# Score products in two fp32r parts, and group pieces inside the value phase, in one layer of a hybrid attention and HGRN2 encoder

## The chip, the cores and the metric

One core of one Trainium2 chip runs the kernel. The metric is the time of one execution on the device in microseconds (us); lower is better. TensorE (PE) multiplies, VectorE (DVE), ScalarE (ACT) and GpSimd (POOL) work element by element, SyncE (SP) issues DMAs.

## The reference, cut to what matters

One layer over 1024 tokens of width 2048: normalise, project by a 2048 x 9216 matrix, run 16 attention heads and 8 HGRN2 heads side by side, gate, project back by `w_out`, add, and close with a gated embedding (`w_pg`, `w_pp`). The change touches the attention alone:

```python
q = rope_partial(heads(aq, ATT_HEADS), pos) * (ATT_HD ** -0.5)
k = rope_partial(heads(ak, ATT_HEADS), pos)
v = heads(av, ATT_HEADS)
res = [dilated_band_attention(q, k, v, w, d) for (w, d) in DILATION_CFG]
outs = jnp.stack([r[0] for r in res])
lses = jnp.stack([r[1] for r in res])
alpha = jax.nn.softmax(lses, axis=0)
o_att = jnp.einsum('gbsh,gbshe->bshe', alpha, outs).reshape(B, S, ATT_W)
y_att = o_att * jax.nn.silu(ag.astype(f32))
```

Each of the 16 heads (64 wide) is seen through three dilated windows, whose results are mixed by their softmax weights. The scores are wanted at float32 accuracy, so the kernel splits queries and keys into parts of lower precision and adds several products.

## The kernel before

The work runs in this order: the values of all heads (`v_group`, to about 360 us), the eight HGRN2 heads (to about 1290), the eight attention pairs of two heads (to about 2100), the output projection and the gated embedding.

A projection of 128 columns is a **group** (`group_parts`, L91 to L110): four weight pieces of 256 KB. Each piece is loaded by SP (L76), cast on ScalarE (`wh`, L83), its rest taken on GpSimd (`wl`, L84), and a bf16 copy made on VectorE (`wb`, L85); three buffers of each. It is written as a generator that yields twice a piece, so that a group can be spread over other work: the first part has 16 products of 512 columns of the high input half (L102, L103; fp32r) and 4 low ones (L107; bf16), the second part 4 low ones. Eight parts make a group, and a ninth call runs its sink, which reads the results out of two PSUM banks (four banks serve the groups, four the other work).

An attention **pair** has a query group, a key group and a gate group. The sinks of queries and keys (`rope_evac`) copy the bank to SBUF (`araw`, L521), turn it by four small DMAs (`apart`), a product on POOL (`apr`) and one on VectorE, and add (L558, L584). Then:

- `keys`, L555 to L574: the sum is split into three bf16 parts, one after the other: cast on ScalarE, subtract on VectorE, twice; the third cast is VectorE's. The two heads of the pair lie in the two halves of the partitions (`nat`), and each part is also copied into the other half by DMA (six copies of 64 KB a half of the tokens).
- `q_half(hf)`, L590 to L608: the queries of one half of the tokens are split likewise into `QT`, whose one buffer is free when the scores of the half before have been computed.
- `scores(hf)`, L626 to L683: eight units, four of stride 4 and wide reach and four local ones. A unit has three bf16 products for each head (L648), which contract both halves of the partitions, then the mask with a row minimum on VectorE (L657) and the exponential on ScalarE (L660). Local units first gather their queries (`aql`, L639), by turns on ScalarE and POOL. After every second unit the method takes one part of a group (`fill`). At its end come the factors of the softmax (L668 to L681).
- `values(hf)`, L685 to L728: eight turns; each scales the probabilities (L701, L703), transposes them on TensorE (L705) and copies them out of PSUM (L708); two turns later their V products run (L717, L720).

The loop at L817 to L836 sets the program order: scores of half 0 with gate parts between, four query parts of the next pair, `q_half(1)`, values of half 0, scores of half 1 with the other query parts, the keys of the next pair, its `q_half(0)`, values of half 1, the gate's other parts. The framework's scheduler takes this order as priority: an instruction whose operands and buffers it expects to be ready may be placed earlier on its engine. Within an engine the order is then fixed. Tiles of `h2` (five buffers of 128 x 512) hold the steps of queries and keys.

Of the kernel before, what the change touches and what calls it, by code (L numbers as in the profile page):

```python
# [13 lines left out]
F32R = mybir.dt.float32r  # L14
# [31 lines left out]
class Kern:  # L46
# [493 lines left out]
    class Pair:  # L540
# [7 lines left out]
        def keys(self):  # L548
            K, nat = self.K, self.nat
            nc = K.nc  # L550
            V = nc.vector
            self.KS = [K.big.tile([128, 2, S], BF16, name=f"ak{i}", tag=t, bufs=n)
                       for i, (t, n) in enumerate((("X", 2), ("X", 2), ("O", 1)))]

            def sink(hf, p):  # L555
                def fin(a, b):
                    kn = K.h2("akn")
                    V.tensor_tensor(kn.rearrange("p (r c) -> p c r", r=4), a.rearrange("p (c r) -> p c r", r=4),  # L558
                                    b.rearrange("p (c r) -> p c r", r=4), op=ALU.add)
                    a = kn  # L560
                    for s in range(3):
                        for h in range(2):
                            n, m = nat[h], nat[1 - h]
                            ks = self.KS[s][:, h].rearrange("p (r c) -> p r c", r=4)[:, :, 128 * hf:128 * hf + 128]
                            kd = ks[n]
                            an = a[n].rearrange("p (r c) -> p r c", r=4)
                            if s < 2:
                                nc.scalar.copy(kd, an)
                                V.tensor_tensor(an, an, kd, op=ALU.subtract)
                                nc.sync.dma_start(ks[m], kd)  # L570
                                if s == 0:
                                    nc.sync.dma_start(self.KS[2][m, h].rearrange("p (r c) -> p r c", r=4)[:, :, 128 * hf:128 * hf + 128], kd)
                            else:
                                V.tensor_copy(kd, an)  # L574
                K.rope_evac(False, hf, p, fin)
            return K.group_parts(self.w_in, 1024 + 128 * self.hp, sink)

# [12 lines left out]
        def q_half(self, hf):  # L590
            K, nat = self.K, self.nat
            nc = K.nc
            V = nc.vector
            q = self.qn[hf]
            QT = K.big.tile([128, 2, 2, 512], BF16, name="aqt", tag="hv", bufs=1)
            self.QT = QT
            for c in range(2):
                cs = slice(256 * c, 256 * c + 256)
                for h in range(2):
                    n = nat[h]  # L600
                    qd = QT[n, h, :, cs]
                    nc.scalar.copy(qd, q[n, None, cs].to_broadcast([64, 2, 256]))
                    V.tensor_tensor(q[n, cs], q[n, cs], QT[n, h, 0, cs], op=ALU.subtract)
                t = K.big.tile([128, 2, 256], BF16, name="aq23", tag="hacc", bufs=1)
                nc.scalar.copy(t[:, 0], q[:, cs])
                V.tensor_tensor(t[:, 1], q[:, cs], t[:, 0], op=ALU.subtract)
                for h in range(2):
                    nc.sync.dma_start(QT[nat[1 - h], h, :, cs], t[nat[h]])  # L608

        def loads(self):  # L610
            K, vsrc = self.K, self.vsrc
# [14 lines left out]
        def scores(self, hf, fill):  # L626
            K, KS, QT = self.K, self.KS, self.QT
            nc = K.nc
            V = nc.vector
            sm = [K.big.tile([128, 2, 4, 256], F32, name=f"asm{h}", tag=("F2", "Q2")[h], bufs=1) for h in range(2)]  # L630
            own = K.sp.tile([128, 2, 2, 2, 4], F32, name="aown", bufs=1)
            oth = K.sp.tile([128, 2, 2, 2, 4], F32, name="aoth", bufs=1)
            for u, (loc, i) in enumerate(((0, 0), (0, 1), (1, 0), (0, 2), (1, 1), (0, 3), (1, 2), (1, 3))):
                w0 = K.wstart(4 * hf + i)
                sc = K.wk("asc")
                if loc:
                    ql = K.big.tile([128, 4, 4, 32], BF16, name="aql", tag="aql", bufs=3)
                    src = QT.rearrange("p h s (r i b) -> p (h s) r i b", i=4, r=4)[:, :, :, i]
                    (nc.gpsimd.tensor_copy if i % 2 else nc.scalar.copy)(ql, src)  # L639
                for h in range(2):  # L640
                    for s, sq in ((0, 0), (1, 0), (2, 1)):
                        if loc:
                            st = ql[:, 2 * h + sq].rearrange("p r b -> p (r b)")
                            mv = KS[s][:, h].rearrange("p (r c) -> p r c", r=4)[:, :, w0 // 4:w0 // 4 + 64]
                        else:
                            st = QT[:, h, sq, 128 * i:128 * i + 128]
                            mv = KS[s][:, h, 256 * i:256 * i + 256]
                        nc.tensor.matmul(sc[:, 256 * h:256 * h + 256], st, mv, start=(h == 0 and s == 0),  # L648
                                         stop=(s == 2), skip_group_check=True)
                if loc:  # L650
                    ms = (w0 - 128 * (4 * hf + i)) // 4 + 32
                    mk = K.MK[:, 384:].rearrange("p (r c) -> p r c", r=4)[:, :, ms:ms + 64]
                else:
                    mk = K.MK[:, 128 - 128 * hf:384 - 128 * hf].rearrange("p (r c) -> p r c", r=4)
                for h in range(2):
                    d = sm[h][:, loc, i]
                    V.tensor_tensor_reduce(out=d.rearrange("p (r c) -> p r c", r=4),  # L657
                                           in0=sc[:, 256 * h:256 * h + 256].rearrange("p (r c) -> p r c", r=4), in1=mk, scale=1.0,
                                           scalar=3.0e38, op0=ALU.add, op1=ALU.min, accum_out=own[:, 0, loc, h, i:i + 1])
                    nc.scalar.activation(d, d, AF.Exp, scale=-1.0, bias=own[:, 0, loc, h, i:i + 1],  # L660
                                         accum_out=own[:, 1, loc, h, i:i + 1])
                if u % 2:
                    next(fill, None)
            for x in range(4):
                for y in range(4):
                    o = oth[32 * x:32 * x + 32].rearrange("p s l h i -> p (s l h) i")[:, :, y]
                    w = own[32 * y:32 * y + 32].rearrange("p s l h i -> p (s l h) i")[:, :, x]
                    V.tensor_copy(o, w)  # L668
            m = K.sp.tile([128, 2, 2, 4], F32, name="afm", bufs=1)
            e = K.sp.tile([128, 2, 2, 2, 4], F32, name="afe", bufs=1)  # L670
            for l in range(2):
                V.tensor_tensor(m[:, l], own[:, 0, l], oth[:, 0, 1 - l], op=ALU.min)
                V.tensor_tensor(e[:, 1, l], m[:, l], oth[:, 0, 1 - l], op=ALU.subtract)
            V.tensor_tensor(e[:, 0], m, own[:, 0], op=ALU.subtract)
            nc.scalar.activation(e, e, AF.Exp)
            V.tensor_tensor(own[:, 1], own[:, 1], e[:, 0], op=ALU.mult)
            for l in range(2):
                V.tensor_tensor(e[:, 1, l], e[:, 1, l], oth[:, 1, 1 - l], op=ALU.mult)
            V.tensor_tensor(m, own[:, 1], e[:, 1], op=ALU.add)
            V.reciprocal(m, m)  # L680
            V.tensor_tensor(m, m, e[:, 0], op=ALU.mult)  # L681
            self.sm[hf] = sm
            self.fac[hf] = m  # L683

        def values(self, hf):  # L685
            K, vn, vc, yt = self.K, self.vn, self.vc, self.yt
            nc = K.nc
            V = nc.vector
# [34 lines left out]
            for n in range(10):  # L723
                if n < 8:
                    turn(n)
                if n >= 2:
                    use(n - 2)
            nc.scalar.copy(yt[:, 512 * hf:512 * hf + 512].rearrange("p (i b r) -> p i r b", i=4, r=4), ov)  # L728
# [16 lines left out]
def tile_hybrid(ctx, tc, x, p, positions, w_in, w_out, g_pre, g_post, g_hg, lb_fwd, lb_bwd, w_pg, w_pp, g_ple, out):  # L745
# [54 lines left out]
    with tc.tile_pool(name="big", bufs=1) as big:  # L800
# [16 lines left out]
        for n, a in enumerate(heads):  # L817
            b = heads[n + 1] if n < 7 else None
            a.loads()
            g = a.gate()  # L820
            if n == 0:
                run(g, 4)
            a.scores(0, g)
            bq = b.queries() if b else iter(())
            run(bq, 4)
            if n == 7:
                run(g, 2)
            a.q_half(1)
            a.values(0)
            a.scores(1, bq if b else islice(g, 2))  # L830
            run(bq)
            if b:
                run(b.keys(), 9)
                b.q_half(0)
            a.values(1)
            run(g)  # L836
    fin = ctx.enter_context(tc.tile_pool(name="fin", bufs=1))
    Y = [fin.tile([128, 4, D], F32, name=f"Y{i}", tag=f"Y{i}") for i in range(2)]
# [256 lines left out]
```

## Time and profile before

| | |
|---|---|
| three runs, us | 2914.51, 2921.52, 2923.47 |
| median, us | 2921.52 |
| the profiled execution, us | 2914.93 |
| its span, first to last instruction, us | 2912.8 |
| mean granted TensorE clock | 0.987 |
| busy, PE / VectorE / ScalarE / GpSimd, us | 2745.8 / 1553.8 / 1019.0 / 1036.4 |

The span is what the trace covers; some 2 us lie around it. A page's L-number is the line of the kernel. A group of instructions is given as line, engine, operation, output<-inputs, shape and count, then busy time and the mean of one, then the idle time of the engine before it with what ended it. TensorE's weight loads are listed apart (PEld) and overlap the products.

### The profile page before, as it was taken

How to read it: one execution, taken by the hardware profiler on the slowest of the kernel's cores; microseconds unless marked ns; L12 is line 12 of the kernel's file. 1: busy time of each engine (PE TensorE's matmuls, PEld its weight loads, DVE VectorE, ACT ScalarE, POOL GpSimd, SP SyncE). 2: the span in 40 equal slices, each digit the busy share in tenths (PEclk: the TensorE clock that was granted, in tenths of full speed). 3: DMA queues.
4: the chain of work that ended last, by engine and by line, in shares of the span. 5: the costliest groups of instructions: out<-in, count | busy, mean ns of one | idle time of the engine just before them, and what ended most of it. 6: DMA issues, size and time to landing. Idle time of an engine off the chain costs nothing. (4 is left out here: it accounts for less than half of the span.)

```text
span 2912.8 us, 45468 instructions
## 1 busy us (share of the span) xinstructions
PE 2745.8 (94%) x17117; PEld 1898.4 (65%) x17360; DVE 1553.8 (53%) x3265; ACT 1019.0 (35%) x2094; POOL 1036.4 (36%) x801
## 2 busy tenths in 40 slices
PE   6999999999999999999899999999899999999997
PEld 4666666676677676676666666666666566566664
DVE  8601116856346346355756566666645635555555
ACT  5311112222122112125556555555633233333323
POOL 3422223313313313322222222233244554666555
PEclk9999999999999999999999999999999999999998
DMA  6412221211111111121222231232344543443453
GB/s 225 122 55 80 76 87 38 66 52 39 57 52 45 51 52 44 53 69 51 77 63 62 71 82 51 66 86 73 98 135 131 161 146 95 127 121 111 145 155 106
DMA packets 279899, 253.08 MB, mean 87 GB/s; under 512 B 46848, under 2 KB 203520, under 8 KB 278528
## 3 DMA queue, kind: packets, MB, share of 16 engines
q1 hardware_dynamic: 270512, 241.24, 28.7%
q10 hardware_dynamic: 9168, 8.93, 0.9%
q8 instruction: 136, 2.23, 0.3%
q14 instruction: 83, 0.68, 0.1%
HBM read 208.16 MB, written 29.36 MB: 82 GB/s over the span
## 5 line engine op out<-in xcount | busy, mean ns | idle before, releaser
L84 POOL TENSOR_TENSOR wl<-raw,wh 128x512 fp32r<-128x512 f32 x568 | 763.6, 1348 | 1580.4 <-ACT wh L83 1528.4
L85 DVE CAST wb<-raw 128x512 bf16<-128x512 f32 x584 | 427.0, 734 | 757.8 <-PE gb L107 252.8
L83 ACT CAST wh<-raw 128x512 fp32r<-128x512 f32 x584 | 358.1, 617 | 1199.1 <-PE gb L102 391.5
L102 PE MATMUL gb<-uh,wh 128*128 128x512 f32 x1792 | 746.0, 416 | 10.3 <-ACT araw L521 6.7
L103 PE MATMUL gb<-uh,wl 128*128 128x512 f32 x1792 | 710.2, 396 | 0.0
L107 PE MATMUL gb<-ul,wb 128*128 128x512 bf16 x1643 | 407.9, 380 | 8.9 <-issue 1.4
L102 PEld LDWEIGHTS gb<-uh,wh 128*128 128x128 f32 x1792 | 338.5, 189 | 99.2 <-ACT araw L521 9.6
L103 PEld LDWEIGHTS gb<-uh,wl 128*128 128x128 f32 x1792 | 338.7, 189 | 69.6
L107 PEld LDWEIGHTS <-wb 128*128 128x128 bf16 x1792 | 157.3, 98 | 207.0 <-issue 57.7
L877 PE MATMUL gb<-wh,yh 128*128 128x512 f32 x512 | 231.1, 452 | 5.7 <-DVE sg L738 4.3
L877 PE MATMUL gb<-wh,th 128*128 128x512 f32 x480 | 214.5, 447 | 0.0
L878 PE MATMUL gb<-wl,yh 128*128 128x512 f32 x512 | 203.4, 398 | 6.3 <-POOL wl L84 6.3
L878 PE MATMUL gb<-wl,th 128*128 128x512 f32 x480 | 189.2, 394 | 6.3 <-POOL wl L84 6.3
L660 ACT ACTIVATE asm<-asm,aown 128x256 f32<-128x256 f32 x256 | 126.9, 498 | 36.7 <-DVE aown L657 36.0
L881 PE MATMUL gb<-wb,yl 128*128 128x512 bf16 x481 | 135.6, 386 | 1.4
L881 PE MATMUL gb<-wb,tl 128*128 128x512 bf16 x452 | 125.3, 382 | 1.0
L877 PEld LDWEIGHTS gb<-wh,yh 128*128 128x128 f32 x512 | 97.8, 191 | 36.6 <-DVE sg L738 5.2
L776 PE MATMUL gb<-wh,uh 128*128 128x512 f32 x256 | 116.6, 462 | 1.4 <-ACT wh L83 1.3
L878 PEld LDWEIGHTS gb<-wl,yh 128*128 128x128 f32 x512 | 97.5, 190 | 27.7 <-POOL wl L84 8.8
L777 PE MATMUL gb<-wl,uh 128*128 128x512 f32 x256 | 102.4, 407 | 9.3 <-POOL wl L84 8.1
L877 PEld LDWEIGHTS gb<-wh,th 128*128 128x128 f32 x480 | 90.8, 189 | 27.2 <-ACT sg L981 2.0
L878 PEld LDWEIGHTS gb<-wl,th 128*128 128x128 f32 x480 | 90.4, 188 | 26.3 <-POOL wl L84 8.9
(287 smaller groups left out, 3798.8 us busy)
## 6 DMA issues: line engine op xcount, KB each, us to landing
raw<-in_w_in_dram SPq DMA_DIRECT2D x320, 256.0 KB
raw<-in_w_out_dram SPq DMA_DIRECT2D x128, 256.0 KB
raw<-in_w_pg_dram SPq DMA_DIRECT2D x128, 256.0 KB
xt<-in_x_dram SPq DMA_DIRECT2D x8, 1024.0 KB
vD<-vo SPq DMA_DIRECT2D x32, 256.0 KB
raw<-yD SPq DMA_DIRECT2D x32, 256.0 KB
xr<-in_x_dram SPq DMA_DIRECT2D x32, 256.0 KB
avn<-vD SPq DMA_DIRECT2D x32, 192.0 KB
```

Source lines behind the costliest of these rows:

```text
L83: nc.scalar.copy(wh, raw)
L84: (sub or nc.gpsimd).tensor_tensor(wl, raw, f32(wh), op=ALU.subtract)
L85: nc.vector.tensor_copy(wb, raw)
L102: nc.tensor.matmul(pb[hf], wh[:, k], self.uh[hf][:, kt], start=(kt == 0), stop=False)
L103: nc.tensor.matmul(pb[hf], wl[:, k], self.uh[hf][:, kt], start=False, stop=False)
L107: mm = nc.tensor.matmul(pb[hf], wb[:, k], self.ul[hf][:, kt], start=False, stop=(kt == KT - 1))
L660: nc.scalar.activation(d, d, AF.Exp, scale=-1.0, bias=own[:, 0, loc, h, i:i + 1], accum_out=own[:, 1, loc, h, i:i + 1])
L776: nc.tensor.matmul(pb[t], hi, wh, start=(k == 0), stop=False)
L777: nc.tensor.matmul(pb[t], hi, wl, start=False, stop=False)
L877: nc.tensor.matmul(pb[t], a, pc[0], start=first, stop=False)
L878: nc.tensor.matmul(pb[t], a, pc[1], start=False, stop=False)
L881: nc.tensor.matmul(pb[t], lo[:, k, 128 * t:128 * t + 128], pc[2], start=False, stop=last)
```

## The change

Queries and keys are split into two fp32r parts (a rounded one and the rest) in place of three bf16 ones. For each head, one key tile holds the high part in one half of the partitions and the low part in the other, and two query tiles hold the high part, and the low part, in both halves; so two products of 128 contracted rows give all four partial products. All rows of these tiles are written by DMA from the split tiles. The local query copies become two for a unit, one on ScalarE and one on POOL. `values` takes a generator and calls it after turns 1 and 5; the loop hands it query or gate parts, and two gate parts move ahead of the next pair's keys.

```diff
--- before.py
+++ after.py
@@ -549,29 +549,21 @@
             K, nat = self.K, self.nat
             nc = K.nc
             V = nc.vector
-            self.KS = [K.big.tile([128, 2, S], BF16, name=f"ak{i}", tag=t, bufs=n)
-                       for i, (t, n) in enumerate((("X", 2), ("X", 2), ("O", 1)))]
+            self.KS = [K.big.tile([128, S], F32R, name=f"ak{h}", tag="X", bufs=2) for h in range(2)]
 
             def sink(hf, p):
                 def fin(a, b):
                     kn = K.h2("akn")
                     V.tensor_tensor(kn.rearrange("p (r c) -> p c r", r=4), a.rearrange("p (c r) -> p c r", r=4),
                                     b.rearrange("p (c r) -> p c r", r=4), op=ALU.add)
-                    a = kn
-                    for s in range(3):
-                        for h in range(2):
-                            n, m = nat[h], nat[1 - h]
-                            ks = self.KS[s][:, h].rearrange("p (r c) -> p r c", r=4)[:, :, 128 * hf:128 * hf + 128]
-                            kd = ks[n]
-                            an = a[n].rearrange("p (r c) -> p r c", r=4)
-                            if s < 2:
-                                nc.scalar.copy(kd, an)
-                                V.tensor_tensor(an, an, kd, op=ALU.subtract)
-                                nc.sync.dma_start(ks[m], kd)
-                                if s == 0:
-                                    nc.sync.dma_start(self.KS[2][m, h].rearrange("p (r c) -> p r c", r=4)[:, :, 128 * hf:128 * hf + 128], kd)
-                            else:
-                                V.tensor_copy(kd, an)
+                    kh = K.h2("akh")
+                    nc.scalar.copy(kh.bitcast(F32R), kn)
+                    V.tensor_tensor(kn.bitcast(F32R), kn, kh, op=ALU.subtract)
+                    for h in range(2):
+                        n, m = nat[h], nat[1 - h]
+                        dst = f32(self.KS[h]).rearrange("p (r c) -> p r c", r=4)[:, :, 128 * hf:128 * hf + 128]
+                        nc.sync.dma_start(dst[n], kh[n].rearrange("p (r c) -> p r c", r=4))
+                        nc.sync.dma_start(dst[m], kn[n].rearrange("p (r c) -> p r c", r=4))
                 K.rope_evac(False, hf, p, fin)
             return K.group_parts(self.w_in, 1024 + 128 * self.hp, sink)
 
@@ -591,21 +583,15 @@
             K, nat = self.K, self.nat
             nc = K.nc
             V = nc.vector
-            q = self.qn[hf]
-            QT = K.big.tile([128, 2, 2, 512], BF16, name="aqt", tag="hv", bufs=1)
-            self.QT = QT
-            for c in range(2):
-                cs = slice(256 * c, 256 * c + 256)
+            q = self.qn.pop(hf)
+            self.QT = [K.big.tile([128, 2, 512], F32R, name=f"aqt{i}", tag=t, bufs=1) for i, t in enumerate(("hv", "O"))]
+            qh = K.h2("aqh")
+            nc.scalar.copy(qh.bitcast(F32R), q)
+            V.tensor_tensor(q.bitcast(F32R), q, qh, op=ALU.subtract)
+            for sq, src in ((0, qh), (1, q)):
                 for h in range(2):
-                    n = nat[h]
-                    qd = QT[n, h, :, cs]
-                    nc.scalar.copy(qd, q[n, None, cs].to_broadcast([64, 2, 256]))
-                    V.tensor_tensor(q[n, cs], q[n, cs], QT[n, h, 0, cs], op=ALU.subtract)
-                t = K.big.tile([128, 2, 256], BF16, name="aq23", tag="hacc", bufs=1)
-                nc.scalar.copy(t[:, 0], q[:, cs])
-                V.tensor_tensor(t[:, 1], q[:, cs], t[:, 0], op=ALU.subtract)
-                for h in range(2):
-                    nc.sync.dma_start(QT[nat[1 - h], h, :, cs], t[nat[h]])
+                    for o in range(2):
+                        nc.sync.dma_start(f32(self.QT[sq])[nat[o], h], src[nat[h]])
 
         def loads(self):
             K, vsrc = self.K, self.vsrc
@@ -634,19 +620,22 @@
                 w0 = K.wstart(4 * hf + i)
                 sc = K.wk("asc")
                 if loc:
-                    ql = K.big.tile([128, 4, 4, 32], BF16, name="aql", tag="aql", bufs=3)
-                    src = QT.rearrange("p h s (r i b) -> p (h s) r i b", i=4, r=4)[:, :, :, i]
-                    (nc.gpsimd.tensor_copy if i % 2 else nc.scalar.copy)(ql, src)
+                    ql = []
+                    for sq in range(2):
+                        tag, n = ("hacc", 1) if i % 2 and sq else ("aql", 3)
+                        ql.append(K.big.tile([128, 2, 4, 32], F32R, name="aql", tag=tag, bufs=n))
+                        src = f32(QT[sq]).rearrange("p h (r i b) -> p h r i b", i=4, r=4)[:, :, :, i]
+                        (nc.gpsimd.tensor_copy if sq else nc.scalar.copy)(ql[sq], src)
                 for h in range(2):
-                    for s, sq in ((0, 0), (1, 0), (2, 1)):
+                    for sq in range(2):
                         if loc:
-                            st = ql[:, 2 * h + sq].rearrange("p r b -> p (r b)")
-                            mv = KS[s][:, h].rearrange("p (r c) -> p r c", r=4)[:, :, w0 // 4:w0 // 4 + 64]
+                            st = ql[sq][:, h].rearrange("p r b -> p (r b)")
+                            mv = KS[h].rearrange("p (r c) -> p r c", r=4)[:, :, w0 // 4:w0 // 4 + 64]
                         else:
-                            st = QT[:, h, sq, 128 * i:128 * i + 128]
-                            mv = KS[s][:, h, 256 * i:256 * i + 256]
-                        nc.tensor.matmul(sc[:, 256 * h:256 * h + 256], st, mv, start=(h == 0 and s == 0),
-                                         stop=(s == 2), skip_group_check=True)
+                            st = QT[sq][:, h, 128 * i:128 * i + 128]
+                            mv = KS[h][:, 256 * i:256 * i + 256]
+                        nc.tensor.matmul(sc[:, 256 * h:256 * h + 256], st, mv, start=(h == 0 and sq == 0),
+                                         stop=(sq == 1), skip_group_check=True)
                 if loc:
                     ms = (w0 - 128 * (4 * hf + i)) // 4 + 32
                     mk = K.MK[:, 384:].rearrange("p (r c) -> p r c", r=4)[:, :, ms:ms + 64]
@@ -682,7 +671,7 @@
             self.sm[hf] = sm
             self.fac[hf] = m
 
-        def values(self, hf):
+        def values(self, hf, fill):
             K, vn, vc, yt = self.K, self.vn, self.vc, self.yt
             nc = K.nc
             V = nc.vector
@@ -723,6 +712,8 @@
             for n in range(10):
                 if n < 8:
                     turn(n)
+                if n in (1, 5):
+                    next(fill, None)
                 if n >= 2:
                     use(n - 2)
             nc.scalar.copy(yt[:, 512 * hf:512 * hf + 512].rearrange("p (i b r) -> p i r b", i=4, r=4), ov)
@@ -823,16 +814,16 @@
             a.scores(0, g)
             bq = b.queries() if b else iter(())
             run(bq, 4)
-            if n == 7:
-                run(g, 2)
             a.q_half(1)
-            a.values(0)
-            a.scores(1, bq if b else islice(g, 2))
+            a.values(0, bq if b else g)
+            a.scores(1, bq if b else islice(g, 1))
             run(bq)
             if b:
+                if n:
+                    run(g, 2)
                 run(b.keys(), 9)
                 b.q_half(0)
-            a.values(1)
+            a.values(1, islice(g, 1 if n == 7 else 2) if n else iter(()))
             run(g)
     fin = ctx.enter_context(tc.tile_pool(name="fin", bufs=1))
     Y = [fin.tile([128, 4, D], F32, name=f"Y{i}", tag=f"Y{i}") for i in range(2)]
```

## The prediction

> **What bounds the kernel now.** I read the page's busy times first, then the attention stage alone, since every edit lies in it: one row of the table of stretches, then the groups of TensorE instructions inside it.
>
> ```profile
> PE 2745.8 (94%) x17117; PEld 1898.4 (65%) x17360; DVE 1553.8 (53%) x3265; ACT 1019.0 (35%) x2094; POOL 1036.4 (36%) x801
> ...
> 1338.59:2034.34 695.75, 649.73 (x3910) 462.87 (x3964) 445.35 (x1315) 393.04 (x951) 179.85 (x151) 0.98 0.25 67
> ...
> L102 PE MATMUL gb<-uh,wh 128*128 128x512 f32 x649 | 273.1, 421 | 10.3 <-ACT araw L521 6.7 <-DVE sg L738 3.5
> L103 PE MATMUL gb<-uh,wl 128*128 128x512 f32 x650 | 259.2, 399 | 0.0
> ...
> L648 PE MATMUL asc<-ak,aql 128*128 128x256 bf16 x336 | 46.3, 284 | 5.1 <-DVE aown L657 5.1
> L648 PE MATMUL asc<-ak,aqt 128*128 128x256 bf16 x336 | 45.5, 276 | 12.2 <-DMA ak<-ak 12.2
> ```
>
> TensorE is busy 94% of the whole, and the stretch from the first score product of pair 0 to that of pair 7 (seven pairs, 695.75 us) shows the same: 649.73 us of TensorE against 445 of VectorE and 393 of ScalarE. But busy time counts each product's modelled end, so I price TensorE by the distance between starts, from the order of time (columns: start, duration of the merged run, instruction, count).
>
> ```profile
> 1402.86 0.39 PE L103 MATMUL gb<-uh,wl 128*128 128x512 f32 x1
> ...
> 1405.60 0.39 PE L103 MATMUL gb<-uh,wl 128*128 128x512 f32 x1
> ...
> 1400.89 1.90 PE L107 MATMUL gb<-ul,wb 128*128 128x512 bf16 x8
> ...
> 1563.78 1.48 PE L648 MATMUL asc<-ak,aqt 128*128 128x256 bf16 x12
> ...
> 1412.75 0.66 PE L705 MATMUL apt<-ident,asm 128*128 128x128 f32 x4
> 1413.34 0.66 PE L717 MATMUL ao<-aPT,avn 128*64 128x128 f32 x8
> ...
> 504.50 0.30 PEld L386 LDWEIGHTS pout<-hvt,ATT 128*128 128x128 f32 x2
> 504.72 0.30 PEld L388 LDWEIGHTS pout<-hst,Q 128*128 128x128 f32 x2
> ```
>
> Twelve steps of high products (fp32r, 512 columns) take 2.74 us: 0.228 each. Eight bf16 products of 512 columns take 1.90 less one duration of 0.38, over seven steps: 0.217. Twelve bf16 score products (256 columns) take 1.48 less one of 0.27, over eleven: 0.110. Four transposes, and the eight instructions of one turn's V products, take 0.59 each. For the seven pairs that is 1299 x 0.228 = 296, half as many low products at 0.217 = 141, 672 x 0.110 = 74, and 112 turns x (0.59 + 0.59) = 132: 643 us of the 696. So this stage is TensorE's own work plus some 53 us in which it is held up or slowed. Who holds it up:
>
> ```profile
> PE asc L648 <- DMA ak<-ak: 14.0, 8, 3.2
> PE apt L705 <- DVE asm L703: 8.7, 4, 2.7
> PE ao L717 <- ACT aPT L708: 8.6, 5, 2.0
> PE gb L102 <- ACT araw L521: 6.7, 7, 1.0
> PE asc L648 <- DVE aown L657: 5.8, 5, 1.8
> PE gb L877 <- DVE sg L738: 4.3, 2, 2.4
> PE gb L102 <- DVE sg L738: 3.5, 1, 3.5
> PE ao L720 <- DVE aPT L708: 2.9, 7, 0.8
> ```
>
> That is the list of waits of TensorE from 1290 to 2090 us (total, times, longest). The first score product of a pair waits for key copies (14.0), V products wait for the transposes' copies out of PSUM (8.6 + 2.9), the first key matmul waits until the query bank is emptied (6.7). The rest of the 53 is the clock, 0.98 over the stretch (14 us), and small steps.
>
> **1. Score products.** Per unit, six bf16 products go and four fp32r products of the same 256 columns come; 128 units in all (two halves x eight units x eight pairs). Now 6 x 0.110 = 0.66 us. No row shows an fp32r product of 256 columns. Lower end: half of the 512-column step, 0.114. The pout rows support it: two loads of 128x128 four-byte weights in 0.22 us, so such a load can follow another in 0.11. Upper end: the load's own duration, 189 ns in the load rows of L102 (98 for bf16), if nothing hides it. I take the bf16 step plus what 512-column fp32r costs over bf16: 0.110 + 0.011 = 0.121, since the load of 189 ns is evidently hidden there to within 11 ns. 4 x 0.121 = 0.48; 0.18 x 128 = **23 us less**. Ends: 0.114 gives 26 less; 0.189 gives 0.76, 13 us more. It falls on the path, because the stage is TensorE's.
>
> The load row weighs against this change, and so does a rule. The Trainium skill, "TensorE: Matmul & The Clock Gate", section "Weight-path perf modes — Fast Weight Load (FWL) and DoubleRow", says the quick weight load is for types other than FP32. The two load durations, 98 and 189 ns, agree. By the rule taken strictly, with 256 columns too few to hide such a load, the term would be the upper end, 13 us more.
>
> **2. Pieces between transposes and V products.** `values` gets two parts of a group: after turn 1 a large one (16 high, 4 low products: 4.5 us), after turn 5 a small one (0.9). The first V products then come 4.5 us after their transposes, where the longest wait was 2.0. I take the 8.6 and most of the 2.9 as gone: **11 us less**. The 8.7 us of transposes waiting for the factors lie ahead of the part, so I leave them. Next late is nothing in `values`: its turns run at 0.59 + 0.59 already.
>
> **3. Queries end earlier.** With two parts in `values(0)`, the queries' last parts and their copy out of PSUM fall inside `scores(1)`, and for pairs 1 to 6 two gate parts (5.4 us) stand before the keys. The wait for `araw` goes at six of seven places: **6 us less**. If the cover went, it would be back at 1 us each.
>
> **4. Key and query preparation.** The rows of groups (count, busy, mean ns, idle before):
>
> ```profile
> L568 ACT CAST ak<-akn 64x512 bf16<-64x512 f32 x64 | 39.5, 617 | 42.1 <-DVE akn L558 31.0 <-DVE akn L569 10.1
> L569 DVE TENSOR_TENSOR akn<-akn,ak 64x512 f32<-64x512 f32 x64 | 58.8, 918 | 15.9 <-ACT ak L568 14.6
> L574 DVE CAST ak<-akn 64x512 bf16<-64x512 f32 x32 | 23.3, 727 | 1.0
> L605 ACT CAST aq<-aq 128x256 bf16<-128x256 f32 x32 | 12.8, 401 | 35.7 <-DMA aqt<-aq 34.1 <-DVE aq L603 1.6
> L639 ACT COPY aql<-aqt 128x512 bf16<-128x512 bf16 x32 | 18.2, 616 | 34.5 <-DMA aqt<-aq 34.5
> ...
> L83 ACT CAST wh<-raw 128x512 fp32r<-128x512 f32 x584 | 358.1, 617 | 1199.1 <-PE gb L102 391.5
> L84 DVE TENSOR_TENSOR wl<-raw,wh 128x512 fp32r<-128x512 f32 x16 | 14.2, 890 | 3.0 <-ACT wh L83 3.0
> ```
>
> A half of keys costs VectorE 4 x 0.92 + 2 x 0.73 = 5.1 us now and one 0.89 after; ScalarE 4 x 0.62 and then one. Queries shrink alike, and ScalarE no longer stands 34 us behind the single buffer of L605. None of it is TensorE's, so off the path it is worth nothing by itself. What it shortens is this chain (pair 2's):
>
> ```profile
> 1601.71 1.24 PE L107 MATMUL gb<-ul,wb 128*128 128x512 bf16 x5
> ...
> 1602.26 0.59 ACT L521 ACTIVATE araw<-gb 128x512 f32<-128x512 f32 x1
> ...
> 1611.14 0.61 ACT L521 ACTIVATE araw<-gb 128x512 f32<-128x512 f32 x1
> ...
> 1616.74 0.70 SPq L525 DMA_DIRECT2D apart<-araw  x1
> ...
> 1625.16 1.08 DVE L558 TENSOR_TENSOR akn<-araw,apr 128x512 f32<-128x512 f32 x1
> ...
> 1632.17 0.44 PE L648 MATMUL asc<-ak,aqt 128*128 128x256 bf16 x2 [2.37 <-DMA ak<-ak]
> ```
>
> From the last key product (1602.8) to the first score, 29.4 us pass: the second half's `araw` is copied at 1611, its rotation is queued on SP behind six key copies, and the split follows from 1626. Afterwards the split is one cast and one subtraction (1.5 us, not two such steps in each of six pieces) and four copies for six; I count the chain 2 to 8 us shorter. But every key row now comes by DMA, 128 KB a copy (64 before), and the cover shrinks: two gate parts that stood behind `values(1)` now stand before the keys, 5.4 us at each of six transitions. The net I take at 1 us lost each: **6 us more**; ends, 14 less (the whole wait goes) and 32 more (6 x 5.4).
>
> SP issues four more copies a pair (24 for 20) at 0.6 to 0.7 us: covered by `values(0)` and the query parts at `q_half(1)`, by the 21 us of key matmuls at `q_half(0)`. Raw weight loads stand behind them on SP; a q_half of eight issues is 5 us, and three raw buffers hold 16 us of matmuls, so nothing. The second-half local query tiles must wait for earlier products, on POOL as now:
>
> ```profile
> POOL aql L639 <- PE asc L648: 28.8, 9, 8.2
> ```
>
> That wait reaches no TensorE row today. Copies double in number and halve in elements (0.40 us by L605); behind a POOL copy stands the subtraction of a weight piece, hidden by the same buffers: nothing. In pair 7 the gate's last small part moves into `values(1)`, and the output stage, which waits for its banks (4.3), may start 3 us earlier or later: nothing.
>
> **Sum.** -23 - 11 - 6 + 6 = **-34 us**. The profiled execution took 2914.93 us (span 2912.8 and 2 around it), the fastest end of the runs; their median, 2921.52, is 6.6 higher. The forecast for the median is 2921.5 - 34 = **2887 us**, its own range 2870 to 2905.
>
> **Rivals.** A: the loads bound the products (0.189): 13 more instead of 23 less, 2923 us, no change. For it, the load rows; against it, the 11 ns of step 1 and the pout rows. This is the Trainium skill's rule on quick loads at work.
>
> B, slower: **the keys come late**. Place: the first score product of pairs 2 to 7. Price: 5.4 us of lost cover at six transitions, 32, and the clock. A wait of 3.5 us after 1428 was followed by this (last columns: granted clock, DMA share, GB/s):
>
> ```profile
> 1430.00:1435.00 5.00, 3.26 (x7) 2.17 (x7) 4.77 (x7) 3.09 (x6) 1.27 (x1) 0.60 0.78 186
> 1435.00:1440.00 5.00, 4.13 (x16) 2.72 (x16) 3.89 (x9) 2.35 (x5) 2.39 (x2) 0.50 0.69 186
> ```
>
> 2.0 + 2.5 = 4.5 us of clock lost, 27 at six places. Then -23 - 11 - 6 + 32 + 27 = +19: 2940 us. It decides once the chain does not shorten while the cover does; the larger copies at a DMA share already 0.7 to 0.8 speak for it, against it that the program's order pulls later gate pieces before the scores (3.4 pieces lie between in pair 2, where two were written). The Trainium skill, same page, Part 1, has the clock halve after an idle window of about 3.4 us; the trace agrees with its 0.50.
>
> C: only the products pay, and moved pieces leave as much wait elsewhere: 2898 us. D: the relief of VectorE and ScalarE removes the waits for factors and keys and half the clock's 14 as well: -34 - 6 - 14 - 7 = -61, 2860 us. E: fp32r gains nothing from 256 columns, 0.228 a product, 32 us more for 23 less: 2942 us; the change then does not do what it says.
>
> **Chances.** Forecast 0.48, A 0.10, B 0.13, C 0.15, D 0.10, E 0.04. Faster by over 0.3% (9 us, about what a measurement of this kernel can tell from no change): forecast, C and D with a little lost at the edge, 0.72; within, A and edges, 0.11; slower, B and E, 0.17. The range 2862 to 2930 leaves out B, E and part of D: near 0.2.
>
> **What would show it.** Step 1: L648's successors 512 in number, about 0.12 us apart; at 0.19 it is A. Step 2: the waits of L717 and L720 gone. Step 3: no wait for `araw` at L102. Step 4: the wait of the first score below 3 us a pair; over 5 us with a clock near 0.5 behind it is B. The forecast is wrong if the order of instructions on TensorE changes so that pieces run out before scores.

## The result, and the profile after

| | before | after |
|---|---|---|
| median of six runs each, taken together, us | 2917.47 | 2904.23 |
| lowest to highest, us | 2914.51 to 2923.47 | 2899.36 to 2906.73 |
| profiled execution, us (its span) | 2914.93 (2912.8) | 2900.24 (2898.5) |
| mean granted TensorE clock | 0.987 | 0.984 |

The ratio is 0.9948, with a 95% interval of 0.9934 to 0.9963: the change makes the kernel faster by 13 us, about 0.5%. The forecast was 34 us faster (2887 us); the time lies inside the range, and the gain is well under half of the forecast one. Each ratio below is to the kernel before as timed beside that run, with medians from 2911.24 to 2915.96 us.

Of the changed kernel's page, the busy times (engine, us, share, instructions); its table of stretches for the attention stage, from the first score product to the last V product, which is the same stretch as the row of before below it (start and end, length, busy PE, PEld, DVE, ACT, POOL, clock, DMA share, GB/s):

```profile
PE 2726.5 (94%) x16853; PEld 1893.5 (65%) x17104; DVE 1449.1 (50%) x3105; ACT 951.3 (33%) x1998; POOL 1047.7 (36%) x833
```

```profile
1341.96:2097.70 755.74, 694.30 (x4069) 500.22 (x4136) 399.45 (x1340) 384.80 (x994) 207.59 (x198) 0.97 0.34 90
```

```profile
1338.59:2098.20 759.61, 704.67 (x4298) 501.75 (x4356) 491.80 (x1482) 441.25 (x1070) 192.55 (x162) 0.98 0.26 69
```

VectorE lost 92 us of work in the stage and ScalarE 56, yet the stage is only 4 us shorter. (Some more of the output projection now falls inside it, so what follows the stage is shorter by about 14.) The list of TensorE's waits from 1290 to 2090 us (engine, tile, line, what it waited for: total, times, longest) answers to the one shown of before:

```profile
PE gb L102 <- DMA aqt<-aqh: 19.7, 4, 5.6
PE apt L694 <- DVE asm L692: 16.3, 10, 2.2
PE asc L637 <- DMA aqt<-aqh: 9.5, 1, 9.5
PE gb L102 <- DVE sg L729: 4.4, 1, 4.4
PE asc L637 <- DMA aqt<-aq: 3.4, 2, 3.1
```

The waits of V products (8.6 and 2.9) and the wait for `araw` (6.7) are gone, as forecast. The wait for key copies (14.0), which was forecast to grow a little, is off the list too, but the query copies are issued behind the key copies and may hide it. In their place stand waits put down to the copies of the *query* tiles: 19.7 + 9.5 + 3.4 = 32.6 us at seven places, where before had none. The transposes' wait for the softmax factors nearly doubled, from 8.7 to 16.3.

The transition that ends with the first score at 1630 shows one of the new waits. (It is that of pair 3, counted from 0, and the same one as the prediction's chain to 1632, which is there called pair 2's; the lines are of the same place.) Of all engines' instructions in order of time, those that matter (start, duration of the merged run, instruction, count, idle time before it and what ended it):

```profile
1588.56 2.18 DVE L576 TENSOR_TENSOR aq<-araw,apr 128x512 f32<-128x512 f32 x1 [2.40 <-POOL apr L528]
...
1621.70 0.62 ACT L560 CAST akh<-akn 128x512 fp32r<-128x512 f32 x1 [3.68 <-DMA avn<-vD]
1622.23 0.62 ACT L589 CAST aqh<-aq 128x512 fp32r<-128x512 f32 x1
...
1622.83 1.90 PE L107 MATMUL gb<-ul,wb 128*128 128x512 bf16 x8
...
1626.94 1.28 ACT L728 ACT_TABLE_LOAD   x1 [3.52 <-DMA ak<-akh]
...
1628.36 2.54 SPq L594 DMA_DIRECT2D aqt<-aq  x4
...
1629.62 0.50 PE L102 MATMUL gb<-uh,wh 128*128 128x512 f32 x1 [4.88 <-DMA aqt<-aqh]
1630.20 0.77 PE L637 MATMUL asc<-ak,aqt 128*128 128x256 f32 x2
```

The later of the two query sums was ready at 1590.7 (1588.56 + 2.18), but the cast that begins the query split (L589) ran only at 1622.2, right behind the cast of the second key half, with no wait of ScalarE between the two. The same holds at all seven transitions. Its eight copies were issued until 1630.9. TensorE had run out of gate parts by then and stood still for 4.9 us. The clock followed:

```profile
1625.00:1630.00 5.00, 0.38 (x1) 0.19 (x1) 1.33 (x3) 2.37 (x3) 0.30 (x1) 1.00 0.84 223
1630.00:1635.00 5.00, 4.92 (x20) 4.18 (x20) 1.06 (x2) 1.23 (x3) 2.96 (x4) 0.66 0.77 239
```

The label "DMA aqt<-aqh" at L102 needs care. L102 there is the first product of the next gate group. It reads no query tile; it needs the bank that the old gate's sink empties, and that sink's sigmoid (L728) stood 3.5 us until a key copy out of `akh` had landed: it writes an `h2` tile too. So two things are late at one place: the gate's sink, and the first score, whose query copies were still being issued then. Both write `h2` tiles; whether that is what holds them, the experiments have to show.

### The profile page after: what moved, and what is told of

It reads as the page before. It is cut to its first block, busy times and chain, and to the rows that moved or that the text cites. A ratio compares the mean times of both kernels' runs of the same rounds, so it can differ in the third digit from the quotient of the medians.

```text
span 2898.5 us, 45014 instructions
## 1 busy us (share of the span) xinstructions
PE 2726.5 (94%) x16853; PEld 1893.5 (65%) x17104; DVE 1449.1 (50%) x3105; ACT 951.3 (33%) x1998; POOL 1047.7 (36%) x833
## 5 line engine op out<-in xcount | busy, mean ns | idle before, releaser
L85 DVE CAST wb<-raw 128x512 bf16<-128x512 f32 x584 | 406.6, 699 | 817.2 <-PE gb L107 311.8
L102 PE MATMUL gb<-uh,wh 128*128 128x512 f32 x1792 | 743.2, 415 | 24.3 <-DMA aqt<-aqh 19.7
L102 PEld LDWEIGHTS gb<-uh,wh 128*128 128x128 f32 x1792 | 339.9, 190 | 110.0 <-DVE sg L729 27.0
```

The lines of the kernel that those rows point to most:

```text
L85: nc.vector.tensor_copy(wb, raw)
L102: nc.tensor.matmul(pb[hf], wh[:, k], self.uh[hf][:, kt], start=(kt == 0), stop=False)
```

## The experiments

Two theories, tried first against each other. **T1, the place of the query split:** `aqh` is a tile of `h2`, whose five buffers seem to be handed out in the order of the program; `q_half(0)` stands behind the keys there, so its split can't begin before the second key half has its tile, however early the queries are ready. **T2, the volume:** eight query copies of 128 KB stand on SP and the DMA engines behind the key copies, and are late for that. All edits are to the changed kernel unless another is named.

### The query half ahead of the keys

```diff
+                b.q_half(0)
                 run(b.keys(), 9)
-                b.q_half(0)
```

> The changed kernel with one order undone: the next pair's first query half is prepared ahead of its keys in program order. Theory 1 (the buffer): the high query part, aqh, takes one of the five h2 buffers, and they are handed out in program order, so it waits behind the two key halves' eight h2 tiles. It expects TensorE's waits on query copies (32.6 us, 7 times) to fall under 5 us, key waits of up to 10 us in their place, and 2875 to 2888 us. Theory 2 (the volume): eight copies of 128 KB are too much for SP and the DMA queues wherever they stand; they now push the key copies back by their 5 us, so the wait returns at the keys with 20 us or more, and the time stays at 2895 to 2906 us.

Measured: **2865.55 us, 0.9829 [0.9808, 0.9851]** against before. The same eight copies and the same `h2` tiles, asked for earlier. Of its trace: ScalarE and TensorE at the same transition.

```profile
1575.50 0.60 ACT L589 CAST aqh<-aq 128x512 fp32r<-128x512 f32 x1
...
1609.69 0.62 ACT L560 CAST akh<-akn 128x512 fp32r<-128x512 f32 x1 [2.86 <-DVE akn L557]
1610.33 1.28 ACT L728 ACT_TABLE_LOAD   x1
...
1614.96 0.36 PE L637 MATMUL asc<-ak,aqt 128*128 128x256 f32 x1 [1.20 <-DMA ak<-akn]
```

The cast came 46.7 us earlier (1575.5 for 1622.2), the gate's sigmoid no longer waits, and the first score follows the second key cast by 5.3 us (8.5 in the changed kernel). Its list of waits:

```profile
PE apt L694 <- DVE asm L692: 15.2, 9, 2.2
PE gb L102 <- DVE sg L729: 6.7, 3, 5.6
PE asc L637 <- DMA ak<-akn: 6.6, 6, 1.4
```

No wait for query copies is left, and the volume of copies is unchanged: T2 falls. The time is 9 us below the range that T1 gave, so T1 has the place and priced it too low.

### No tile of its own for the high query part

```diff
-            qh = K.h2("aqh")
-            nc.scalar.copy(qh.bitcast(F32R), q)
...
+            Q0, Q1 = self.QT
+            for h in range(2):
+                nc.scalar.copy(Q0[nat[h], h], q[nat[h]])
+                V.tensor_tensor(q[nat[h]].bitcast(F32R), q[nat[h]], f32(Q0)[nat[h], h], op=ALU.subtract)
+                nc.sync.dma_start(f32(Q0)[nat[1 - h], h], f32(Q0)[nat[h], h])
```

The low part goes by four copies as before; the keys stay first in the program.

> The changed kernel in its own order (keys first), but the high query part is written straight into the query tile, so that no h2 buffer is asked for; six copies of 128 KB are left of eight. Theory 1 (the buffer) expects the preparation to move ahead of the keys by itself, the waits on query copies to fall under 5 us, and 2875 to 2888 us. Theory 2 (the volume) expects three quarters of the wait to stay, some 24 us, and 2896 to 2903 us.

Measured: **2862.52 us, 0.9825 [0.9801, 0.9849]**. ScalarE in order of time:

```profile
1566.11 1.25 ACT L590 CAST aqt<-aq 64x512 fp32r<-64x512 f32 x2
...
1584.82 0.60 ACT L521 ACTIVATE araw<-gb 128x512 f32<-128x512 f32 x1 [0.44 <-PE gb L107]
```

The place in the program is that of the changed kernel, the tile is another (and two copies fewer go), and the split now runs ahead of the first key bank's copy. The time is below T1's range here too. With the run before, which kept the tile and changed the place, this ties the delay to the two together, as T1 has it: an `h2` tile asked for behind the keys. (How buffers are handed out is inferred from these runs; no view shows it.)

### One buffer's worth of `h2` back

If the number of buffers were short, one `h2` tile fewer in each half of queries and keys should help; if the order in which tiles are asked for decides, it should not.

```diff
-        pr = self.h2("apr")
+        pr = pt
```

> The changed kernel, with its late query part in h2 and its own order, but the rotated product apr is formed in place in its own tile, so that queries and keys ask for four h2 tiles fewer in a pair. Theory 1 (the five h2 buffers run out at the keys; the high query part and then the gate's sigmoid, which empties the banks for the next gate pieces, wait for them) expects a good part of the 43 us that separate this kernel from no_aqh to come back: 2865 to 2890 us, with the wait before the first score of a pair (5 us) under 3 us. Its rival (it is the place of the query part in program order and not the number of buffers) expects under 5 us of gain: 2899 to 2907 us.

Measured: 2904.36 us, 0.9973 [0.996, 0.9986], no gain over the changed kernel. The waits for query copies and for the gate's sink before the first scores come to 36.3 us in its list, for 37.0 in the changed kernel's. ScalarE:

```profile
1622.27 0.62 ACT L560 CAST akh<-akn 128x512 fp32r<-128x512 f32 x1 [3.71 <-DVE akn L557]
1622.80 0.62 ACT L589 CAST aqh<-aq 128x512 fp32r<-128x512 f32 x1
```

The query cast still runs right behind the second key cast: order, not number. The same edit beside the removed tile:

> The same in-place product in the kernel whose high query part is written straight into the query tile. If buffers are no longer short there, nothing is left to gain: 2859 to 2867 us. If they still are, the second half of the keys starts earlier and the waits for key copies (10.5 us) go: 2848 to 2857 us.

Measured: 2862.45 us, 0.983 [0.9805, 0.9855], the same as without it, and the wait for key copies stays (10.4 us for 10.5). The last two runs were timed side by side: between them the late tile costs 42 us.

### The two halves of the change, each alone

The two-part split and products with the loop and `values` of before:

```diff
-                if n in (1, 5):
-                    next(fill, None)
...
-            a.values(0, bq if b else g)
+            a.values(0, iter(()))
...
-                if n:
-                    run(g, 2)
```

> The fp32r parts and two products alone; the loop and the value phase are those of the kernel before, with no group pieces between transposes and V products. Score products 24 us less; the waits at V products (11.5) and at the first key matmul (6.7) are back; four gate parts stand behind the second values, 5.4 us of cover more than in the changed kernel, about the size of each of its waits on queries, so these fall to under 8 us in all. Sum by theory 1 and by theory 2 alike: 2885 to 2898 us.

Measured: **2871.17 us, 0.9854 [0.9831, 0.9877]**. Its list of waits:

```profile
PE asc L637 <- DMA aqt<-aqh: 19.7, 7, 9.4
PE apt L694 <- DVE asm L692: 12.0, 9, 3.0
PE gb L102 <- ACT araw L521: 3.7, 6, 0.6
```

The time is 14 us below the expected range. V products wait for nothing here, without a piece between them and their transposes: the two-part split with its products was enough (which part of it does this, no run separates). The query wait is there too, far above the 8 us expected, but with more cover behind the keys it comes to 19.7 us.

The pieces alone, put into the kernel before with its bf16 operands (the diff's lines in `values` and in the loop, nothing else):

> The group pieces and the new loop alone, on three bf16 parts and three products. The waits at V products and at the first key matmul go (18 us), the factors are waited for 8 us longer, and the chain of the keys, which is as long as before, has 5.4 us less cover at six transitions (32 us, to which the clock may add). Query halves ask for no h2 buffer here, so theory 1 expects no wait on query copies. Sum: 2917 to 2940 us, no gain or slower.

Measured: **2930.89 us, 1.0055 [1.0034, 1.0076]: slower.** Its list of waits goes to 2130 us, since its attention stage ends at 2118:

```profile
PE apt L705 <- DVE asm L703: 23.8, 9, 5.8
PE asc L648 <- DMA ak<-ak: 15.7, 8, 3.2
PE asc L648 <- DVE aown L657: 11.3, 7, 2.1
PE gb L102 <- DVE sg L740: 3.5, 1, 3.5
PE ao L720 <- DVE aPT L708: 2.4, 7, 0.5
```

The pieces did shorten the waits of the V products (8.6 + 2.9 before, 2.4 here) and took away that for `araw` (6.7), and as much or more was lost at other places: the transposes' wait rose by 14.9 (from 8.9 over the same stretch of before), that of the scores for the row minimum by 5.5, that for keys by 1.7. So the time lies in the expected range by luck: it was to come from the keys (32 us), and came mostly from elsewhere. That the parts were missed where they had stood before is the likely reason; no run puts them back one by one.

### Do the pieces pay once the queries are early?

`split_alone` with the query half ahead of the keys, to be held against `q_first`:

```diff
+                b.q_half(0)
                 run(b.keys(), 9)
-                b.q_half(0)
```

> The fp32r parts and two products in the loop of the kernel before (no group pieces in the value phase), with the next pair's first query half ahead of its keys. It asks what the moved pieces are worth once the query wait is gone. If they pay (theory of the prediction: 18 us at V products and at the first key matmul), this is slower than the same order with the pieces (2865.6 us) by 5 us or more. If they only take cover from the chain of the keys and from the factors (the rival, the pieces alone having cost 15 us), it is faster than that by 5 us or more: 2848 to 2860 us.

Measured: 2873.85 us, 0.9864 [0.9849, 0.9878].

```profile
PE asc L637 <- DMA ak<-akh: 15.3, 6, 3.0
PE apt L694 <- DVE asm L692: 9.0, 4, 4.1
PE gb L102 <- ACT araw L521: 5.1, 7, 1.3
```

In this loop the early query half gains nothing: the keys are the next late thing. In the changed loop it gains some 35 us (0.9948 to 0.9829, of 2916). With the queries early the pieces are worth some 10 us (0.9864 to 0.9829, though the two intervals just touch), with the queries late they cost 27 (0.9854 to 0.9948). Why the keys wait longer here than in `q_first`, with more cover behind them, no run tells.

### The transposes' wait

This wait had become the longest one left. One theory was that the exponentials and the factors stood behind the local query copies on ScalarE. The edit moves the fourth local unit's high copy to POOL.

```diff
-                        (nc.gpsimd.tensor_copy if sq else nc.scalar.copy)(ql[sq], src)
+                        (nc.gpsimd.tensor_copy if sq or i == 3 else nc.scalar.copy)(ql[sq], src)
```

> The changed kernel with one assignment changed: both query copies of the fourth local unit of a half are made on POOL (ScalarE made one of them). Theory: the waits of transposes for the factors (16.3 us, 10 times; 8.7 before) come from the fourth local unit, whose ScalarE copy stands behind some 14 exponentials; with it on POOL the unit runs 4 to 5 us earlier, ScalarE ends its exponentials 1.5 to 2 us earlier, the waits fall to under 8 us, and the time to 2890 to 2898 us. Rival: ScalarE's 16 exponentials set the factors however the units are fed; the waits stay above 13 us, 2901 to 2907 us.

Measured: 2906.98 us, 0.9976 [0.9967, 0.9985].

```profile
PE gb L102 <- DVE sg L729: 15.7, 3, 5.4
PE apt L694 <- DVE asm L692: 12.3, 9, 2.3
PE asc L637 <- DMA aqt<-aqh: 9.5, 1, 9.5
PE gb L102 <- DMA aqt<-aqh: 9.1, 2, 4.6
PE asc L637 <- issue: 4.1, 2, 2.6
PE asc L637 <- ACT aql L628: 3.6, 1, 3.6
...
PE gb L102 <- ACT araw L521: 3.3, 2, 2.9
```

(To 2130 us, since this stage ends at 2104.) The wait fell from 16.3 to 12.3, between the two expectations (the time lies in the rival's range), so the copies seem to be part of it. The time didn't fall: the waits at the transitions, for the queries and the gate's sink, hardly moved (15.7 + 9.5 + 9.1 = 34.3 us, for 37.0), and waits for a local query copy (3.6), for `araw` (3.3) and of kind "issue" (4.1 for 1.2) came in addition. This list also shows the label at L102 split in two (15.7 by `sg`, 9.1 by query copies), which bears out the caution above. The same edit with the query half first:

> The changed kernel with the first query half ahead of the keys and the fourth local copies on POOL. If the two waits are independent, 2865.6 less 6 to 12 us: 2853 to 2860 us; if exponentials set the factors, 2863 to 2868 us.

Measured: 2869.89 us, 0.9852 [0.9836, 0.9869]: 4 us above `q_first` by the medians, with the transposes' wait at 10.8 (15.2) and that of L102 for `sg` at 9.4 (6.7). No gain there either, and a time above both expected ranges. What would remove this wait stays open.

### The runs in one table

For each profiled execution: the change of the span against 2912.8; the score products at their step inside a run at full clock (128 x (0.66 - 4 x 0.118) = 24 us less, see below), the same figure for every version; the total of the list of TensorE's waits from 1290 to 2130 us, and its change; and the rest. The clock is the mean of the whole execution.

| | span | products | waits (before: 55) | rest | clock |
|---|---|---|---|---|---|
| changed kernel | -14 | -24 | 61: +6 | +4 | 0.984 |
| `q_first` | -54 | -24 | 34: -21 | -9 | 0.990 |
| `no_aqh` | -53 | -24 | 35: -20 | -9 | 0.991 |
| `split_alone` | -45 | -24 | 41: -14 | -7 | 0.988 |
| `split_q_first` | -42 | -24 | 40: -15 | -3 | 0.986 |
| `fill_alone` | +17 | 0 | 59: +4 | +13 | 0.983 |
| `no_apr` | -11 | -24 | 65: +10 | +4 | 0.983 |
| `no_aqh_no_apr` | -49 | -24 | 35: -20 | -5 | 0.990 |
| `i3_pool` | -6 | -24 | 65: +9 | +9 | 0.981 |
| `q_first_i3` | -46 | -24 | 38: -17 | -5 | 0.990 |

By and large the rest is lower where the clock is higher (0.987 before), in no fixed share; it also holds what the products lost of their 24 us, see step 1. What differs most between the versions is waiting, and the clock beside it. Each row is one execution, so a few us either way say nothing. The best versions, `no_aqh`, `q_first` and `no_aqh_no_apr`, beat both kernels by more than 1% and can't be told apart from one another.

## Why the prediction was right in direction and wrong in size

**Step 1, the products (-23): the step is right, the sum too large.** Of the changed kernel, two runs of them in order of time; the row of their tile (count with this operand, duration in ns least/median/greatest, first and last start); and the group of the loads for the local units:

```profile
1571.38 0.64 PE L637 MATMUL asc<-ak,aql 128*128 128x256 f32 x4
...
1633.61 0.87 PE L637 MATMUL asc<-ak,aqt 128*128 128x256 f32 x6
```

```profile
L637 PE MATMUL asc<-ak,aqt x256: 274/282/553, 1342.0 to 2073.8; 128*128 128x256 f32 x128
```

```profile
L637 PEld LDWEIGHTS asc<-ak,aql 128*128 128x128 f32 x256 | 38.2, 195 | 10.4 <-ACT aql L628 7.2 <-POOL aql L628 0.3
```

Six products take 0.87 less one duration of 0.28, over five steps: 0.118 each (0.121 was taken). The products number 512, 256 by each operand. That is the step inside a run at full clock, and the median over all of them. Taken from every start in the trace to the next (waits above 0.15 us left out), the mean step is 0.143 in the changed kernel and 0.132 in `no_aqh`, for 0.113 before: 14 and 20 us less instead of 23. Many first steps of a run take 0.21 to 0.30 us, and the steps right behind the late first scores run at half clock (granted clock 0.50 from 1630.0 to 1633.4 us). Rival A would have had 0.189, and E 0.228; neither came. The list of loads says why their duration was no bound: 256 loads of 195 ns would fill 49.9 us one after the other, but busy time is 38.2, so loads overlap each other. The Trainium skill's rule on quick loads ("TensorE: Matmul & The Clock Gate", section "Weight-path perf modes — Fast Weight Load (FWL) and DoubleRow") holds for the length of a load, 195 ns here beside 98 for bf16; the loss that the prediction made of it, taken strictly, isn't there inside a run.

**Step 2, the V products (-11): right in amount, but not the pieces' alone.** Their waits went to nothing, but they go in `split_alone` too, without the pieces; the pieces alone bring them from 11.5 to 2.4 (`fill_alone`). And the sentence on the transposes' 8.7 us ("I leave them") failed: with the pieces that wait is 16.3 (12.0 without), likely because parts that stood ahead of the factors were moved behind them. In the bf16 kernel the pieces gave back elsewhere all of the V products' waits.

**Step 3, the wait for `araw` (-6): right**, and in good part by the pieces: it isn't on the list any more, and is 3.7 and 5.1 in the two versions without them.

**Step 4, keys and queries (+6): this is the step that failed.** The keys themselves went better than taken: where late queries don't hide it, their wait is 6.6 (`q_first`) or 10.5 (`no_aqh`), for 14.0 before, so 4 to 7 us less and not 6 more. What failed is the cost of nothing for the query copies, "covered by `values(0)` and the query parts at `q_half(1)`, by the 21 us of key matmuls at `q_half(0)`". The key matmuls cover only work that can start beside them, and the query split couldn't: it takes an `h2` tile behind those of the keys. So 32.6 us of waits for query copies stand at seven places, and the gate parts ran out before the first scores, the sign that the prediction itself had named for being wrong. Before, it wrote straight into the query tile, and did run beside the key matmuls:

```profile
1588.06 1.90 ACT L602 CAST aqt<-aq 64x512 bf16<-64x512 f32 x3 [1.07 <-DVE aq L584]
```

Its cost in the changed loop is 35 us by the ratio of `q_first` and 36 by that of `no_aqh` (0.9948 less 0.9829 or 0.9825, of 2916); by the bare medians 39 and 42, and 37 and 42 in the two pairs timed side by side (`i3_pool` and `q_first_i3`, `no_apr` and `no_aqh_no_apr`). Without that loss the sum of -34 would have been too cautious: these two versions are 50 and 51 us faster than before by their ratios. What was left out there on the good side is in part the relief that rival D named: waits are 20 us shorter in all, where steps 2 to 4 add up to 11, and the clock is higher (0.990 and 0.991 for 0.987); the wait for the factors, which D had as gone, is longer. That the changed kernel's time still fell inside the range is luck: the loss that was left out and these gains offset each other in part.

**The rivals.** The time came out nearest to C (2898), and its mechanism is half of what happened: the products pay (14 us rather than 23), and more wait than was removed stands elsewhere (61 us for 55); it isn't the moved pieces alone that leave it, though. B had the right place and the right shape (TensorE stands still for some 4 to 6 us before most pairs, and the clock is down behind it) but on the queries instead of the keys, and its price of 59 us, 27 of them clock, was too high. The Trainium skill, "TensorE: Matmul & The Clock Gate", Part 1, has the clock fall after such an idle stretch; the trace agrees with 0.66 in the 5 us after 4.9 us of standing still.

## What to carry to other kernels

When an edit gives an intermediate value a tile from a shared set of buffers, look at where in the program that tile is asked for and what stands ahead of it: being ready early is worth nothing if the buffer comes late, and here that one tile ate more than two thirds of what the change could give. Cover named for a step counts only if the step can start beside it, so look for the step's first instruction in the trace, not only for the engine time around it. And a piece moved into one gap is taken from another: price the place that it leaves as well.

## What the runs showed of the hardware that was not expected

- An fp32r product of 256 columns with a fresh 128x128 load follows another inside a run in 0.118 us, though each load is listed at 195 ns; a bf16 one took 0.110.
- Other time, lost clock with it, goes beside waiting in no fixed share (the column "rest"): 21 us less waiting came with 9 us less of the rest in `q_first`, 4 us more waiting with 13 more in `fill_alone`, where the stage's clock was 0.96:

```profile
1339.10:2118.40 779.30, 723.17 (x4373) 507.07 (x4375) 487.11 (x1486) 441.09 (x1072) 199.58 (x164) 0.96 0.25 68
```

- The share of the DMA engines rose from 0.26 to 0.34 in the stage with the larger and more numerous copies, and to 0.35 in `q_first`, below: the copies' volume was not what made them late.

```profile
1339.40:2057.10 717.70, 686.56 (x4123) 493.54 (x4124) 400.89 (x1338) 380.23 (x990) 207.38 (x197) 0.99 0.35 94
```
